# Two running sums of weights share tiles in another way, and the products that read them change places

## The chip, the cores and the metric

The kernel runs on one core of one Trainium2 chip. The metric is the device time of one execution in microseconds (us), the median of several. A core has TensorE (PE: matmuls into the accumulator banks of PSUM), VectorE (DVE), ScalarE (ACT), GpSimd (POOL) and SyncE (SP); the engines run their own queues in order and wait for each other by semaphores. DMA transfers are issued from an engine's queue, here SyncE's and GpSimd's.

## The reference

The reference is a decoder trunk of two layers on 512 tokens of width 1024, all in float32. Layer 0 mixes with differential and block-sparse attention, layer 1 with gated linear attention. Each layer ends with the part that the change touches, a feed-forward net of width 4096:

```python
def sqrelu_mlp(x, w1, w2):
    return jnp.square(jax.nn.relu(x @ w1)) @ w2

# in each layer
x = layer_norm(DEEPNORM_ALPHA * x + mix, ln_mix_g[l], ln_mix_b[l])
x = layer_norm(DEEPNORM_ALPHA * x + sqrelu_mlp(x, w1[l], w2[l]), ln_ffn_g[l], ln_ffn_b[l])
```

## The kernel before

**Split operands.** To keep float32 accuracy, each operand of a matmul is split into a high part (ScalarE, L117) and the rest (VectorE, L118). One product of two operands is then three matmuls: high by high, high by rest, rest by high. A weight tile is loaded whole into `raw` (four buffers, SyncE, L169), and its two parts go into buffers `w`: eight single ones, of which an entry of two takes two, and in the feed-forward stage one more double one. `entries` lists the splits in the order of use; `pump` starts the next one when a product has released its weights. `load_to` issues loads four ahead, as far as `raw` has a free buffer.

**The feed-forward net.** `ffn` works in four blocks of 1024 hidden columns. Blocks 0 to 2 multiply 2 x 2 matrices of sub-matrices with seven products in place of eight (Winograd's form), for the first matrix with `pair` (L872 to L918) on groups of columns, and for the second matrix with `second()` (L927 to L990). Block 3 has pairs too, and ends in plain products. Block 0 has one pair, blocks 1 to 3 have four each; a pair is 84 matmuls `pp` (L881). For a pair, `add_pair` forms sums of its two `raw` tiles on VectorE (L194, L187) and splits them; the results of a pair are added into `hb` in L815.

**Seven products.** In `second()` a product is 24 matmuls `pf` (L944): a left operand `ho` (a split of a quarter of `hb` or of a sum of such quarters: o11, o1, o12, o4, o2, o3, o22) by a right operand in two halves. The right operands are, with q00, q01, q10, q11 for the four quarters of the block of the second matrix: q00, q00+q01, q10, q11, q00+q01+q11, q01+q11 and the sum of all four. The results gather in bank pairs `A`, `B` and `C`: after a product, `into_x` (L403 or L405, VectorE) adds what the banks hold to x, and a later product adds on to the same banks. With `by_tokens` a product finishes the first 128 tokens before the second, and releases its two weight halves at its end; without it, it finishes and releases half by half. So a product on the banks of the one before it must wait for `into_x`.

**The sums.** The running sums of quarters are made by DMA, in tiles `ws` of 2 x 1024 columns (two of them, from the pool of eight large tiles that also holds `hb`). GpSimd issues a plain transfer (L225) and then transfers that add to what the tile holds (L230); `keep_in_program_order` keeps their order. `start_sums` runs at the start of a block and makes q00+q01 in the first tile and q01+q11 in the second. After a half of the first tile has been split, `summed` adds the next quarter to it: q11 behind the second product's split, q10 behind the fifth's. An add waits until what it adds to has landed, and until the split has read the tile.

**The order.** A planner at compile time orders each engine's instructions: of those that it believes to be ready it takes the one that stands first in the program, by durations of its own. That order is then fixed on each engine.

Of the kernel before, what the change touches and what calls it, by code (L numbers as in the profile page):

```python
# [16 lines left out]
ALU = mybir.AluOpType  # L17
AX = mybir.AxisListType

P = 128  # L20
# [27 lines left out]
def trunk(ctx, tc, a, out):  # L48
    nc = tc.nc
    V, A, G, PE = nc.vector, nc.scalar, nc.gpsimd, nc.tensor  # L50
# [9 lines left out]
    def bank(name="ps"):  # L60
        return psp.tile([P, 512], F32, tag="ps", name=name)
# [11 lines left out]
    def t8(name, shape=(P, NH, T), dt=F32):  # L73
        return pool["u"].tile(list(shape), dt, tag="u", name=name)

    def t4(name, shape=(P, 1024), dt=F32):
        return pool["h"].tile(list(shape), dt, tag="h", name=name)
# [38 lines left out]
    def split(h, l, src):  # L116
        A.activation(h, src, AF.Copy)  # L117
        V.tensor_tensor(l, src, h.bitcast(F32), op=ALU.subtract)  # L118
# [27 lines left out]
    def pump(n=1):  # L146
        while n and W["ready"] < len(entries) and room(entries[W["ready"]][1]):
            ready()
            n -= 1

    def nxt():
        if not ops:
            ready()
        c, h, l = ops.popleft()
        held.append(c)
        return c, h, l

    def release(c):
        held.remove(c)
        W[c[0]] -= c[1]  # L160
# [6 lines left out]
    def add_load(dst, src):  # L167

        loads.append(lambda: nc.sync.dma_start(dst(), src))  # L169
        return len(loads)  # L170

    def raw(key):
        def dst():
            got[key] = rp.tile([P, 1024], F32, tag="raw", name="raw")
            return got[key]
        return dst
# [36 lines left out]
    def quad(u, i, n, half):  # L213

        return wst[u + 4 * i + 2 * n + half]

    tsum = {}

    def start_sums(key):

        u = blocks[key]
        tsum[key] = [t8("ws", (P, 2, 1024)) for _ in range(2)]
        for t, i in zip(tsum[key], (0, 1)):
            for half in range(2):
                tc.keep_in_program_order(nc.gpsimd.dma_start(t[:, half], quad(u, 0, 1, half)))  # L225
            for half in range(2):
                add_quad(t[:, half], quad(u, i, i, half))

    def add_quad(t, src):
        tc.keep_in_program_order(nc.gpsimd.dma_start(t, src, accum_op=ALU.add))  # L230
# [3 lines left out]
    def add_block(u, key):  # L234

        blocks[key] = u

        def plain(i, n):
            r = []
            for half in range(2):  # L240
                k = add_load(raw((key, i, n, half)), quad(u, i, n, half))
                r.append((k, 2, lambda h, l, half=half: split(h, l, got.pop((key, i, n, half)))))
            return r

        def summed(m, then=None):
            def fn(half, h, l):
                t = tsum[key][m][:, half]
                split(h, l, t)
                if then:
                    add_quad(t, quad(u, *then, half))  # L250
            return [(len(loads), 2, lambda h, l, half=half: fn(half, h, l)) for half in range(2)]

        steps = (lambda: plain(0, 0), lambda: summed(0, (1, 1)), lambda: plain(1, 0), lambda: plain(1, 1),
                 lambda: summed(0, (1, 0)), lambda: summed(1), lambda: summed(0))
        return [e for st in steps for e in st()]

    def add_ffn(u, layer):
        for b in range(NB):
            add_units(u, PLAIN[b])
            first, second = [], []  # L260
            for j in range(PLAIN[b], FBLK, 2):
                first += add_pair(u + j)
            if b < NB - 1:
                second = add_block(u + FBLK, (layer, b))
            entries.extend(first + second)
            if b == NB - 1:
                add_units(u + FBLK, FBLK)
            u += 2 * FBLK
# [131 lines left out]
    def resid(t, h, ps, scale, acc=None, op=ALU.add):  # L400
        xs = x[:, t, h * 512:(h + 1) * 512]
        if scale is None and acc is None:
            V.tensor_tensor(xs, xs, ps, op=op)  # L403
        else:
            V.scalar_tensor_tensor(xs, xs, 1.0 if scale is None else scale, ps, op0=ALU.mult, op1=op,  # L405
                                   accum_out=None if acc is None else acc[t][:, h:h + 1])
# [192 lines left out]
    xs, ws, done = set(), [set(), set()], [set(), set()]  # L599
# [201 lines left out]
    steps = [diff_step(h, t) for h in range(NH) for t in range(NT)]  # L801
# [10 lines left out]
    def ffn(layer, last, nfirst, c0, t_last):  # L812
# [109 lines left out]
        def into_x(i, n, bs):  # L922
            for tt in range(2):
                resid(2 * i + tt, n, bs[tt], None if (i, n) in seen else ALPHA, op=ALU.subtract if n else ALU.add)
            seen.add((i, n))

        def second():  # L927


            c = {k: [bank("pf") for _ in range(2)] for k in "AC"}  # L930
            a11, a21, a12, a22 = H[0][:, 0], H[0][:, 1], H[1][:, 0], H[1][:, 1]

            def left(src, halves=False):
                h, l = (t4("ho", (P, 4, 256), F32R) for _ in range(2))
                for z in ((slice(0, 2), slice(2, 4)) if halves else (slice(0, 4),)):
                    split(h[:, z], l[:, z], src[:, z])
                return h, l

            def one(k, op, w, half, tt, first):
                r = [z.rearrange("p (j c) -> p j c", j=2) for z in w[1:]]  # L940
                for j in range(2):
                    l = [z[:, 2 * half + j, tt * P:(tt + 1) * P] for z in op]
                    for n, (x_, y_) in enumerate(((0, 0), (0, 1), (1, 0))):
                        PE.matmul(c[k][tt], l[x_], r[y_][:, j, :], start=first and half == j == n == 0,  # L944
                                  stop=half == j == 1 and n == 2, skip_group_check=True)

            def prod(k, op, first, by_tokens=False):
                if by_tokens:
                    w = [nxt() for _ in range(2)]
                    for tt in range(2):  # L950
                        for half in range(2):
                            one(k, op, w[half], half, tt, first)
                            if tt == 1:
                                release(w[half][0])
                                pump(2)
                    return
                for half in range(2):
                    w = nxt()
                    for tt in range(2):
                        one(k, op, w, half, tt, first)  # L960
                    release(w[0])
                    pump(2)

            o11 = left(a11, True)
            s = t4("s", (P, 4, 256))
            sub(s, a22, a21)
            o1 = left(s)
            prod("A", o11, True)
            into_x(0, 0, c["A"])
            o12 = left(a12)  # L970
            V.scalar_tensor_tensor(s, s, -1.0, a11, op0=ALU.mult, op1=ALU.subtract)
            V.scalar_tensor_tensor(a12, a12, -1.0, s, op0=ALU.mult, op1=ALU.subtract)
            prod("C", o1, True)
            into_x(1, 1, c["C"])
            o4 = left(a12)
            c["B"] = [bank("pf") for _ in range(2)]
            prod("B", o12, True)
            into_x(0, 0, c["B"])
            o2 = left(s)
            sub(a21, a11, a21)  # L980
            prod("C", o4, False)
            into_x(0, 1, c["C"])
            o3 = left(a21)
            prod("A", o2, False, True)
            into_x(0, 1, c["A"])
            o22 = left(a22)
            prod("A", o3, False, True)
            into_x(1, 1, c["A"])
            prod("A", o22, False, True)
            into_x(1, 0, c["A"])  # L990
# [7 lines left out]
        for b in range(NB):  # L998
# [3 lines left out]
            if not fin:  # L1002
                start_sums((layer, b))
            for n in range(0 if b else nfirst, PLAIN[b]):
                add_a(evac(n))
            if b == 0:
                ops_, third = right_operands()
# [5 lines left out]
            if not fin:  # L1013
                second()
                continue
# [398 lines left out]
```

## Time and profile before

| | us |
|---|---|
| median of 3 runs | 1190.36 (1188.38 to 1193.89) |
| profiled execution | 1192.47 |
| its span, first to last instruction | 1190.7 |

| engine | busy us | share |
|---|---|---|
| TensorE, matmuls | 1140.6 | 96% |
| TensorE, weight loads | 988.1 | 83% |
| VectorE | 867.8 | 73% |
| ScalarE | 622.8 | 52% |
| GpSimd | 112.2 | 9% |

The three runs and the profiled execution are of one program; the profiled execution's rows are used below. An engine's busy time is not enough to tell what sets the end: matmuls are pipelined, and a wait on an engine that has time left costs nothing. So the views that count are those of waits and the timelines of single stretches. Times in them are counted from the span's start. In layer 0, `second()` of blocks 0, 1 and 2 starts at 297, 385 and 470 us.

### The profile page before, as it was taken

How to read it: one execution, taken by the hardware profiler on the slowest of the kernel's cores; microseconds unless marked ns; L12 is line 12 of the kernel's file. 1: busy time of each engine (PE TensorE's matmuls, PEld its weight loads, DVE VectorE, ACT ScalarE, POOL GpSimd, SP SyncE). 2: the span in 40 equal slices, each digit the busy share in tenths (PEclk: the TensorE clock that was granted, in tenths of full speed). 3: DMA queues.
4: the chain of work that ended last, by engine and by line, in shares of the span. 5: the costliest groups of instructions: out<-in, count | busy, mean ns of one | idle time of the engine just before them, and what ended most of it. 6: DMA issues, size and time to landing. Idle time of an engine off the chain costs nothing.

```text
span 1190.7 us, 16757 instructions
## 1 busy us (share of the span) xinstructions
PE 1140.6 (96%) x6538; PEld 988.1 (83%) x6538; DVE 867.8 (73%) x1359; ACT 622.8 (52%) x1046; POOL 112.2 (9%) x136
## 2 busy tenths in 40 slices
PE   9999999999989999999999999999999899899997
PEld 6787776889779789799888888888987887887986
DVE  5677863578976986995657756486879679679846
ACT  6535466446646647566336433633564565564731
POOL 1132410010110010001010000000102002000000
PEclk9999999999999999999999999999999999899998
DMA  7512242073674675435232123401656566463331
GB/s 265 205 53 71 71 147 66 1 212 94 139 210 121 141 200 142 107 106 188 72 102 84 58 87 99 138 32 50 181 159 161 140 163 174 125 168 66 121 107 71
DMA packets 42735, 145.79 MB, mean 122 GB/s; under 512 B 5152, under 2 KB 6176, under 8 KB 42656
## 3 DMA queue, kind: packets, MB, share of 16 engines
q1 hardware_dynamic: 30640, 101.92, 26.3%
q0 software_dynamic: 12016, 42.80, 16.5%
q8 instruction: 51, 0.84, 0.3%
q14 instruction: 28, 0.23, 0.1%
HBM read 142.61 MB, written 2.10 MB: 122 GB/s over the span
## 4 chain that ended last, share of the span: by engine, by line
PE 79%; DVE 6%; ACT 6%; issue 4%; DMA 3%; POOL 1%; DVEq 0%; POOLq 0%; ACTq 0%
PE pp L881 20%; PE pf L944 15%; PE pf L280 4%; PE pf L279 4%; PE pf L281 4%; PE pb L279 4%; PE pb L280 4%; PE pb L281 3%; PE pa L279 3%; PE pa L281 3%; PE pa L280 3%; DMA raw<-in_wst 3%; ACT w L117 2%; DVE w L118 2%; PE pl L1212 1%
## 5 line engine op out<-in xcount | busy, mean ns | idle before, releaser
L118 DVE TENSOR_TENSOR w<-raw,w 128x1024 fp32r<-128x1024 f32 (+2 forms) x210 | 242.6, 1165 | 122.5 <-ACT w L117 99.4
L117 ACT ACTIVATE w<-raw 128x1024 fp32r<-128x1024 f32 (+2 forms) x210 | 205.7, 986 | 167.1 <-PE pf L944 26.9
L944 PE MATMUL pf<-w,ho 128*128 128x512 f32 x1008 | 234.9, 391 | 4.9 <-ACT ho L117 4.0
L944 PEld LDWEIGHTS pf<-w,ho 128*128 128x128 f32 x1008 | 187.4, 188 | 48.0 <-ACT ho L117 6.6
L881 PE MATMUL pp<-xTh,w 128*128 128x256 f32 x832 | 161.3, 286 | 9.3 <-ACT w L117 5.8
L881 PEld LDWEIGHTS pp<-xTh,w 128*128 128x128 f32 x832 | 135.6, 194 | 12.1 <-ACT w L117 7.5
L881 PE MATMUL pp<-T,w 128*128 128x256 f32 x936 | 127.1, 289 | 14.9 <-DVE hb L815 14.9
L881 PEld LDWEIGHTS pp<-T,w 128*128 128x128 f32 x936 | 119.2, 196 | 16.8 <-DVE hb L815 15.7
L881 PE MATMUL pp<-xTl,w 128*128 128x256 f32 x416 | 118.9, 286 | 0.0
L279 PE MATMUL pa<-xTh,w 128*128 128x512 f32 x264 | 106.0, 403 | 0.0
L281 PE MATMUL pa<-xTh,w 128*128 128x512 f32 x264 | 103.1, 391 | 0.0
L280 PE MATMUL pa<-xTl,w 128*128 128x512 f32 x264 | 103.0, 390 | 0.0
L881 PEld LDWEIGHTS pp<-xTl,w 128*128 128x128 f32 x416 | 81.0, 195 | 0.2
L230 POOL DMA_DIRECT2D ws<-in_wst x48 | 42.1, 877 | 400.5 <-DVE w L118 334.8
L279 PE MATMUL pb<-w,xTh 128*128 128x512 f32 x192 | 76.3, 401 | 1.0 <-ACT w L117 1.0
L280 PE MATMUL pb<-w,xTh 128*128 128x512 f32 x192 | 75.1, 391 | 0.4 <-DVE w L118 0.4
L281 PE MATMUL pb<-w,xTl 128*128 128x512 f32 x192 | 75.3, 392 | 0.0
L117 ACT ACTIVATE w<-ws 128x1024 fp32r<-128x1024 f32 x48 | 50.8, 1059 | 42.4 <-PE pf L944 41.6
L118 DVE TENSOR_TENSOR w<-ws,w 128x1024 fp32r<-128x1024 f32 x48 | 58.1, 1220 | 14.0 <-ACT w L117 9.2
L281 PEld LDWEIGHTS pa<-xTh,w 128*128 128x128 f32 x264 | 49.6, 188 | 10.6
L280 PEld LDWEIGHTS pa<-xTl,w 128*128 128x128 f32 x264 | 49.8, 188 | 9.2
L279 PEld LDWEIGHTS pa<-xTh,w 128*128 128x128 f32 x264 | 49.7, 189 | 9.1
(280 smaller groups left out, 2082.5 us busy)
## 6 DMA issues: line engine op xcount, KB each, us to landing
raw<-in_wst SPq DMA_DIRECT2D x178, 512.0 KB, 3.6
ws<-in_wst POOLq DMA_DIRECT2D x72, 512.0 KB, 6.0
xraw<-in_xT SPq DMA_DIRECT2D x8, 256.0 KB, 4.9
x<-in_x SPq DMA_DIRECT2D x4, 512.0 KB, 6.8
gb<-in_lng POOLq DMA_DIRECT2D x4, 512.0 KB, 5.6
gb<-in_lnb POOLq DMA_DIRECT2D x4, 512.0 KB, 6.5
out_x<-x SPq DMA_DIRECT2D x7, 256.0 KB, 2.0
tab<-in_rope SPq DMA_DIRECT2D x2, 512.0 KB, 5.2
```

Of the source, the lines that this page charges most:

```text
L117: A.activation(h, src, AF.Copy)
L118: V.tensor_tensor(l, src, h.bitcast(F32), op=ALU.subtract)
L230: tc.keep_in_program_order(nc.gpsimd.dma_start(t, src, accum_op=ALU.add))
L279: PE.matmul(o, l[0], r[0], start=first, stop=False)
L280: PE.matmul(o, l[0], r[1], start=False, stop=False)
L281: PE.matmul(o, l[1], r[0], start=False, stop=last)
L881: PE.matmul(o, w[x_], z[y_], start=first and k == n == 0, stop=k == 3 and n == 2, skip_group_check=True)
L944: PE.matmul(c[k][tt], l[x_], r[y_][:, j, :], start=first and half == j == n == 0, stop=half == j == 1 and n == 2, skip_group_check=True)
L1212: PE.matmul(pl[:, h * P:(h + 1) * P], z, z, start=True, stop=True)
```

## The change

`start_sums` makes q00+q01 in the first tile as before. The second tile is first a copy of the first by DMA, and then q11 is added to it: q00+q01+q11. Once the second product's operand has been split from the first tile, `third` writes q01 there anew and adds q11. After the second tile has been split, q10 is added to it, which makes the sum of all four. So the first tile is read for q00+q01 and q01+q11, the second for q00+q01+q11 and the sum of four.

The order of products changes to match: the product of o2 with q00+q01+q11 (banks `A`) comes fourth, no longer by tokens, and that of o4 with q11 (banks `C`) fifth. The other five keep their places. The negated sum in `a12` (L972) is formed after the second product's `into_x`, and o2 is split before o4.

```diff
     def start_sums(key):
 
         u = blocks[key]
-        tsum[key] = [t8("ws", (P, 2, 1024)) for _ in range(2)]
-        for t, i in zip(tsum[key], (0, 1)):
-            for half in range(2):
-                tc.keep_in_program_order(nc.gpsimd.dma_start(t[:, half], quad(u, 0, 1, half)))
-            for half in range(2):
-                add_quad(t[:, half], quad(u, i, i, half))
+        a1, a2 = tsum[key] = [t8("ws", (P, 2, 1024)) for _ in range(2)]
+        for half in range(2):
+            bring(a1[:, half], quad(u, 0, 1, half))
+        for half in range(2):
+            add_quad(a1[:, half], quad(u, 0, 0, half))
+        for half in range(2):
+            bring(a2[:, half], a1[:, half])
+        for half in range(2):
+            add_quad(a2[:, half], quad(u, 1, 1, half))
+
+    def bring(t, src):
+        tc.keep_in_program_order(nc.gpsimd.dma_start(t, src))
...
                 if then:
-                    add_quad(t, quad(u, *then, half))
+                    then(t, half)
...
-        steps = (lambda: plain(0, 0), lambda: summed(0, (1, 1)), lambda: plain(1, 0), lambda: plain(1, 1),
-                 lambda: summed(0, (1, 0)), lambda: summed(1), lambda: summed(0))
+        def third(t, half):
+            bring(t, quad(u, 0, 1, half))
+            add_quad(t, quad(u, 1, 1, half))
+
+        steps = (lambda: plain(0, 0), lambda: summed(0, third), lambda: plain(1, 0),
+                 lambda: summed(1, lambda t, half: add_quad(t, quad(u, 1, 0, half))),
+                 lambda: plain(1, 1), lambda: summed(0), lambda: summed(1))
...
             V.scalar_tensor_tensor(s, s, -1.0, a11, op0=ALU.mult, op1=ALU.subtract)
-            V.scalar_tensor_tensor(a12, a12, -1.0, s, op0=ALU.mult, op1=ALU.subtract)
             prod("C", o1, True)
             into_x(1, 1, c["C"])
-            o4 = left(a12)
+            V.scalar_tensor_tensor(a12, a12, -1.0, s, op0=ALU.mult, op1=ALU.subtract)
+            o2 = left(s)
             c["B"] = [bank("pf") for _ in range(2)]
             prod("B", o12, True)
             into_x(0, 0, c["B"])
-            o2 = left(s)
+            o4 = left(a12)
             sub(a21, a11, a21)
+            prod("A", o2, False)
+            into_x(0, 1, c["A"])
+            o3 = left(a21)
             prod("C", o4, False)
             into_x(0, 1, c["C"])
-            o3 = left(a21)
-            prod("A", o2, False, True)
-            into_x(0, 1, c["A"])
             o22 = left(a22)
             prod("A", o3, False, True)
             into_x(1, 1, c["A"])
```

## Rows read from the trace of the kernel before

**Rows 1.** The page's first part: busy us (share) x instructions.

```profile
PE 1140.6 (96%) x6538; PEld 988.1 (83%) x6538; DVE 867.8 (73%) x1359; ACT 622.8 (52%) x1046; POOL 112.2 (9%) x136
```

**Rows 2.** Waits of TensorE, whole span: us in total, times, longest.

```profile
PE pp L881 <- DVE hb L815: 14.9, 4, 4.3
PE pp L881 <- ACT w L117: 5.8, 4, 1.5
...
PE pp L881 <- DVE w L118: 3.5, 2, 1.7
```

**Rows 3.** Timeline of TensorE, 408 to 439: start, us, [idle before <-releaser].

```profile
408.68 5.60 PE L944 MATMUL pf<-w,ho 128*128 128x512 f32 x24
...
416.24 0.50 PE L881 MATMUL pp<-xTh,w 128*128 128x256 f32 x2 [1.73 <-DVE w L118]
...
417.06 11.07 PE L944 MATMUL pf<-w,ho 128*128 128x512 f32 x48
...
438.41 0.86 PE L881 MATMUL pp<-T,w 128*128 128x256 f32 x5 [2.62 <-DVE hb L815]
```

**Rows 4.** Timeline of VectorE, 400 to 439, same block.

```profile
401.75 1.21 DVE L118 TENSOR_TENSOR ho<-hb,ho 128x1024 fp32r<-128x1024 f32 x1
...
412.38 1.22 DVE L118 TENSOR_TENSOR ho<-hb,ho 128x1024 fp32r<-128x1024 f32 x1
...
416.10 1.28 DVE L403 TENSOR_TENSOR x<-x,pf 128x512 f32<-128x512 f32 x2
...
418.43 1.28 DVE L194 TENSOR_TENSOR s<-raw 128x512 f32<-128x512 f32 x2
...
434.60 0.69 DVE L194 TENSOR_TENSOR s<-raw 128x512 f32<-128x512 f32 x1 [3.17 <-DMA raw<-in_wst]
```

**Rows 5.** Single issues at 339.9, 388.0, 427.9, 428.5, 513.5: KB, us to landing.

```profile
raw<-in_wst SPq DMA_DIRECT2D x1, 512.0 KB, 7.8
...
raw<-in_wst SPq DMA_DIRECT2D x1, 512.0 KB, 4.7
...
raw<-in_wst SPq DMA_DIRECT2D x1, 512.0 KB, 6.7
...
raw<-in_wst SPq DMA_DIRECT2D x1, 512.0 KB, 9.9
...
raw<-in_wst SPq DMA_DIRECT2D x1, 512.0 KB, 3.5
```

**Rows 6.** Timeline of GpSimd, 380 to 442: its DMA issues.

```profile
385.75 0.87 POOL L230 DMA_DIRECT2D ws<-in_wst  x1 [2.14 <-DVE w L118]
...
404.40 0.87 POOL L230 DMA_DIRECT2D ws<-in_wst  x1 [2.60 <-DVE w L118]
413.90 1.09 POOL L225 DMA_DIRECT2D ws<-in_wst  x2 [8.63 <-DVE ho L118]
...
427.83 1.92 POOL L230 DMA_DIRECT2D ws<-in_wst  x2 [6.62 <-DMA ws<-in_wst]
```

**Rows 7.** Timeline of ScalarE, 407 to 414.

```profile
412.73 1.06 ACT L117 ACTIVATE w<-ws 128x1024 fp32r<-128x1024 f32 x1 [1.12 <-PE pf L944]
```

**Rows 8.** Issue to landing, L225 (24 plain transfers), then L230 (48 adds).

```profile
DMA to landing us min/median/max: 3.8/6.9/9.5
...
DMA to landing us min/median/max: 5.3/5.8/10.4
```

**Rows 9.** Timeline of TensorE, the start of `second()` in block 2.

```profile
470.43 2.91 PE L944 MATMUL pf<-w,ho 128*128 128x512 f32 x12
```

**Rows 10.** Windows: length, busy us of PE, PEld, DVE, ACT, POOL, PEclk, DMA share.

```profile
388.50:431.40 42.90, 40.45 (x193) 33.76 (x194) 42.12 (x49) 22.76 (x26) 7.48 (x10) 1.00 0.69 178
...
352.00:357.00 5.00, 4.99 (x30) 4.99 (x31) 3.20 (x5) 4.05 (x8) 0.00 (x0) 0.68 0.60 210
438.40:443.40 5.00, 4.99 (x41) 4.99 (x42) 3.60 (x6) 4.46 (x10) 0.00 (x0) 1.00 0.39 108
1022.10:1028.10 6.00, 5.97 (x29) 5.97 (x30) 3.45 (x6) 3.74 (x8) 0.00 (x0) 0.54 0.30 90
```

## The prediction, made blind

> **What bounds the kernel now.** The page's first part comes before anything else: TensorE is busy for 96% of the span, VectorE for 73% [rows 1]. A transfer, split or sum is worth something here only if it shortens TensorE's 50 us of idle time, so the next view is whom TensorE waited for [rows 2]. The feed-forward blocks hold 24 us of it: four waits for the adds to `hb` in L815 (14.9 us) and six for the first weight of a pair (5.8 + 3.5 us). No entry names a weight sum. That is the first thing to see: the tile `ws`, which the change rearranges, is not what TensorE waits for.
>
> The timelines place these waits. In `second()` of block 1, layer 0, the fifth product is the 24 matmuls from 408.68 to 414.28. Then a few matmuls of the next pair are slipped in, one of them waits 1.73 us for its weight, and the sixth product starts only at 417.06 [rows 3]. What slipped them in: the fifth product (bank `A`, o2) and the sixth (`A`, o3) add into the same banks, and between the two `into_x` must read them. VectorE reaches that L403 at 416.10, since a split of `ho` from 412.38 and weight splits stand ahead of it [rows 4]. There are six such gaps, 9.3 us, one for each block with a `second()` [rows 2].
>
> The other wait comes 8 us after the seventh product, which ends at 428 [rows 3]. VectorE stands at L194 for 3.17 us until a `raw` tile lands [rows 4]; the adds of L815 are behind it in VectorE's queue, and TensorE waits 2.62 us for those [rows 3]. That transfer (427.9) took 6.7 us, its like in block 0 (339.9) 7.8 us; at the start of block 3 (513.5), which makes no sums, one took 3.5 us [rows 5]. GpSimd's row shows what moved meanwhile: the last two adds of `start_sums`, from 427.83 [rows 6].
>
> **The change part by part.** *Sums.* Before, a block has 12 transfers of 512 KB: four plain and eight adds. After, 14: two plain ones of q01, two copies of `a1` into `a2`, two more of q01 in `third`, and still eight adds. On the readers' side this removes a tight step: the add issued at 404.40 behind the fifth product's split lands within 5.8 us (median), at 410.2, and its reader, the split at 412.73, waited for TensorE and not for it [rows 6 to 8]. There were 2.5 us to spare, so relaxing this gains 0. The new distances are longer: `a2` is split for the fourth product and again for the seventh, three products of 5.6 us later; `a1` for the second and the sixth, 22 us apart, in which a plain transfer (3.8 to 9.5 us) and an add (5.3 to 10.4) fit even at their worst [rows 8]. In `third` the second half's transfer stands on GpSimd's queue behind the first half's add, about 4 us; only sums wait there.
>
> *The copy in start_sums.* It waits for `a1`'s add, and `a2`'s add waits for it; on GpSimd's queue only the second copy and the adds stand behind. The trace has no copy from one on-chip tile to another. By the nearest rows it takes 3.8 us (a plain transfer alone) to 9.5 (one in a crowd) [rows 8]; I take 4.5, near the first, since one other transfer at most is ahead of it. The chain is then 4.5 + 6 + 4.5 + 6 = 21 us from its first issue. Before, the last adds are issued 14 us after it, 413.90 to 427.83 [rows 6], and need 6 to 10 more [rows 8]: it ends about when it did. The first reader of `a2` comes after the four pairs, 428 to 470 [rows 3, 9]; they hide the chain with 20 us to spare, and all four links at their upper ends (9.5 + 10.4, twice: 40 us) would just be covered. Without the pairs all 21 us would be paid. Exposed is only what these transfers do to the `raw` loads.
>
> *The order of products.* o2 moves to fourth, o4 to fifth. `into_x` can now read `A` during a whole product `C`, 5.6 us, and the sixth product can follow the fifth at once, provided that o3 is split: it was at 413.6, and the fifth product ended at 414.28 [rows 3, 4]. The fourth product needs o2 where it needed o4; o4's split ended at 402.96, just ahead of the fourth product's start at 403.1 (408.68 less 5.6) [rows 3, 4]. o2 comes from `s`, one operation earlier than `a12`, so it is no later: 0. L972 behind an `into_x` delays o4, which has a product more: 0. The fourth and fifth products now both release their weights by halves; one slot comes free 1.4 us earlier, a help inside the next term.
>
> *Term 1, the six gaps.* If they go entirely, TensorE saves 9.3 us, and in the four blocks with an L815 wait the slipped-in matmuls, about 1 us each, fill time in which TensorE waited anyway: upper end 13. But VectorE is busy for 42.12 of the 42.90 us from 388.50 to 431.40 [rows 10]. In the old order it can be 0.78 us earlier and no more, and a TensorE that comes early waits for L815 instead: lower end 6 x 0.78 = 4.7. The order need not stay: before some L403s VectorE does sums of a later pair (L194 at 418.43) [rows 4] that can wait. I take 7, midway between 4.7 and 9.3.
>
> *Term 2, the L815 waits.* They end with the landing of a `raw` tile. At its issue, two adds and another `raw` were under way; after the change, the tail of the second copy, an add or two and the same `raw`. Bounds: it lands as without sums, 3.5 us (all 14.9 us go), or as the worst `raw` of the stretch (428.5), 9.9 us, 3.2 more at each of four places (+13) [rows 5]. Nothing in the count of transfers favours either strongly; I take 0.5 us each, 2 us. The Trainium skill has a rule that speaks against even this: in "DMA: Bandwidth & Descriptors", section "Queues, rings and completion order", each DMA engine goes round the queues that have work, packet by packet, so how many transfers wait in one queue would not matter to the other; by that rule this term is 0 and the sum 2 us poorer. The trace agrees only in part: beside a single add (385.75) a `raw` (388.0) took 4.7 us, beside two 6.7 [rows 5, 6].
>
> *Term 3, the clock.* After the long waits the granted clock lay between its two levels of 2.4 and 1.2 GHz: 0.68 over 5 us and 0.54 over 6, which is 1.6 and 2.8 us lost; after the 2.62 us wait it stayed at 1.00 [rows 10]. The fourth place counts as the first: 6.0 us in all. Waits somewhat shorter give back a part: I take 0.5 us (bounds: 6 gained, 2 lost).
>
> Sum: -7 - 2 - 0.5 = -9.5 us. The profiled execution took 1192.47 us, 1190.7 of them span; after it would be 1183.0. The median of the three runs lies 2.1 us below that execution, so I predict 1181.
>
> **The rivals.**
> *VectorE is the bound (A).* The gaps go and the time returns as longer waits for L815; 0.78 us a block is left, 1185 to 1188, say 1187. For it: the busy time in [rows 10]. Against it: part of the work in the way can come later.
> *Every wait goes (B).* `raw` lands in 3.5 us, VectorE keeps up, the clock stays: 9.3 + 14.9 + 6 = 30 us, 1160. Against it: `a2`'s adds are still issued about when the `raw` is.
> *Slower (C).* The copy reads and writes the same memory that `raw` is written to, and the serial chain shifts its transfers onto that one load. If it lands in over 9 us instead of 6.7 to 7.8, the four waits grow by 3.2 each: +13, +2 of clock, less term 1's 7: +8, 1198. For it: a `raw` issued 0.6 us later already took 9.9 [rows 5]. Below 8 us it costs nothing that counts.
> *It does nothing (D).* The sums were not late, and the compile-time planner keeps matmuls of a pair, with a weight that is late, ahead of the sixth product: 1190, give or take 3.
>
> **How the numbers follow.** Forecast 0.42, A 0.25, B 0.10, C 0.10, D 0.13. A change under 0.5% (6 us) can't be told from none in this kernel. Faster: nearly all of the forecast, B and a little of A, 0.53. Slower: C and a sliver of D, 0.11. The rest, 0.36, is no difference. The range leaves out B and C: from 1168 (term 1 at 13, terms 2 and 3 at 9 together) to 1193 (D's upper end).
>
> **What would show it.** After the change the six waits of `pp` for a weight are gone and the sixth product follows the fifth without a gap; waits for L815 remain at the same four places with 2 to 4 us; the copies land in 4 to 6 us; no split waits for `ws`. If the gaps are gone and L815's waits have grown by as much, A holds; if that `raw` lands in over 9 us, C. I am wrong from the start if matmuls of a pair still stand between the fifth and the sixth product, or if a fourth product waits for `ho`.

## The result, and the profile after

| us | before | after |
|---|---|---|
| median | 1191.57 (4 runs, 1188.38 to 1193.89) | 1176.72 (4 runs, 1175.88 to 1177.74) |
| profiled execution | 1192.47 | 1176.95 |
| its span | 1190.7 | 1175.2 |

The ratio of the medians is 0.9878, 95% interval 0.9851 to 0.9904: 14.9 us or 1.2% faster, 4.3 us below the predicted 1181. The lines of the kernel after stand 11 lower: L815 is L826, L881 is L892, L944 is L955; plain transfers and copies of `ws` are L233, adds L236.

A stretch is named here by the block whose `second()` opens it; the pairs behind that `second()` belong to the next block. The page's first part answers to [rows 1], the waits of TensorE in the feed-forward stage (us in total, times, longest) to [rows 2].

```profile
PE 1140.5 (97%) x6538; PEld 988.6 (84%) x6538; DVE 867.2 (74%) x1359; ACT 622.5 (53%) x1046; POOL 119.5 (10%) x148
```

```profile
PE pp L892 <- DVE hb L826: 8.8, 4, 3.6
PE pf L955 <- ACT ho L117: 4.0, 6, 0.8
PE ds L1269 <- DVE S L1271: 0.7, 1, 0.7
```

TensorE, VectorE and ScalarE are busy for as long as before, GpSimd 7.3 us longer; what went is idle time. The two entries of `pp` for a weight are gone (5.8 + 3.5 us), and the waits for the adds to `hb` fell from 14.9 to 8.8 us. The timeline of TensorE in block 1's stretch, layer 0 (start, us, [idle before <-releaser]) answers to [rows 3]:

```profile
388.69 29.32 PE L955 MATMUL pf<-w,ho 128*128 128x512 f32 x128
...
418.32 5.63 PE L955 MATMUL pf<-w,ho 128*128 128x512 f32 x24
...
424.74 3.04 PE L892 MATMUL pp<-T,w 128*128 128x256 f32 x24
...
443.04 1.70 PE L892 MATMUL pp<-T,w 128*128 128x256 f32 x12 [0.83 <-DVE hb L826]
```

Before, a few `pp` and a wait of 1.73 us stood between the fifth product and the sixth. Now the 128 matmuls from 388.69 (16 of the first product's stand ahead of them) run through to the end of the sixth, with no `pp` among them; the row of 418.32 is the seventh. What is left of the wait for `hb` comes at 443, 19 us after the seventh product and one pair later than before. VectorE shows why (answers to [rows 4]):

```profile
431.45 0.75 DVE L826 TENSOR_TENSOR hb<-p,pp 128x256 f32<-128x256 f32 x2
...
432.48 0.69 DVE L194 TENSOR_TENSOR s<-raw 128x512 f32<-128x512 f32 x1
...
438.09 0.69 DVE L194 TENSOR_TENSOR s<-raw 128x512 f32<-128x512 f32 x1 [1.52 <-DMA raw<-in_wst]
...
442.24 0.75 DVE L826 TENSOR_TENSOR hb<-p,pp 128x256 f32<-128x256 f32 x2
```

Before, the L194 that waited for a late `raw` was the third pair's, and the first pair's adds to `hb` stood behind it. After, those adds (431.45) stand ahead of the third pair's L194 (432.48), which finds its tile there. The L194 that waits, 1.52 us, is now the fourth pair's, and the second pair's adds (442.24) stand behind it.

**The account.** One window, called the stage below, runs from the first `second()` in layer 0 to the plain products of block 3 in layer 1: 297.43 to 1138.60 before, 300.03 to 1123.07 after. Columns as in [rows 10], with the kernel before first:

```profile
297.43:1138.60 841.17, 810.48 (x4822) 716.98 (x4821) 637.33 (x921) 447.34 (x704) 61.43 (x92) 0.99 0.46 127
```

```profile
300.03:1123.07 823.04, 808.00 (x4822) 715.91 (x4821) 636.75 (x921) 447.11 (x704) 69.02 (x104) 0.99 0.49 138
```

The stage got 18.1 us shorter. TensorE's idle time in it (length less busy) fell from 30.69 to 15.04, by 15.65: the gaps' 9.3, the `hb` waits' 6.1, and 0.2. Its busy time fell by 2.5, with the same 4822 matmuls. The missing 2.6 us between 18.1 and the span's 15.5 lie ahead of the stage, which began at 300.03 and not at 297.43, though the engines run the same instructions in the same order up to 231 us. The granted clock differs (after):

```profile
100.00:140.00 40.00, 37.18 (x182) 29.96 (x181) 30.51 (x57) 20.30 (x45) 14.59 (x8) 0.96 0.22 65
...
180.00:231.00 51.00, 48.68 (x267) 38.47 (x266) 21.20 (x54) 29.90 (x76) 0.00 (x0) 0.97 0.13 39
```

Before:

```profile
100.00:140.00 40.00, 37.26 (x191) 30.19 (x190) 30.45 (x57) 20.31 (x45) 14.58 (x8) 1.00 0.19 63
180.00:228.60 48.60, 46.73 (x265) 37.30 (x266) 19.75 (x52) 28.52 (x73) 0.00 (x0) 1.00 0.11 33
```

In the other profiles the stage began between 297.2 and 300.3 us, with the old sums as with the new, so this is a difference of executions. Profiles are therefore compared below by their waits and by the time from the stage's start to the end of the span: 893.3 us before, 875.1 after.

### The profile page after: what moved, and what is told of

It is laid out like the page before. It is cut to its first block, busy times and chain, and to the rows that moved or that the text cites. A ratio compares the mean times of both kernels' runs of the same rounds, so it can differ in the third digit from the quotient of the medians.

```text
span 1175.2 us, 16786 instructions
## 1 busy us (share of the span) xinstructions
PE 1140.5 (97%) x6538; PEld 988.6 (84%) x6538; DVE 867.2 (74%) x1359; ACT 622.5 (53%) x1046; POOL 119.5 (10%) x148
## 4 chain that ended last, share of the span: by engine, by line
PE 80%; DVE 6%; ACT 5%; issue 4%; DMA 3%; POOL 1%; DVEq 0%; ACTq 0%; POOLq 0%
PE pf L955 18%; PE pp L892 18%; PE pf L291 4%; PE pf L290 4%; PE pf L292 4%; PE pb L290 4%; PE pb L291 4%; PE pb L292 4%; PE pa L290 3%; DMA raw<-in_wst 3%; PE pa L291 3%; PE pa L292 3%; DVE w L118 2%; ACT w L117 2%; PE pl L1223 1%
## 5 line engine op out<-in xcount | busy, mean ns | idle before, releaser
L955 PE MATMUL pf<-w,ho 128*128 128x512 f32 x1008 | 234.6, 391 | 4.9 <-ACT ho L117 4.0
L955 PEld LDWEIGHTS pf<-w,ho 128*128 128x128 f32 x1008 | 187.4, 188 | 48.1 <-ACT ho L117 6.6
L892 PE MATMUL pp<-xTh,w 128*128 128x256 f32 x832 | 159.8, 285 | 0.0
L892 PEld LDWEIGHTS pp<-xTh,w 128*128 128x128 f32 x832 | 134.7, 194 | 0.5
L892 PE MATMUL pp<-T,w 128*128 128x256 f32 x936 | 126.3, 289 | 8.8 <-DVE hb L826 8.8
L892 PEld LDWEIGHTS pp<-T,w 128*128 128x128 f32 x936 | 118.7, 195 | 11.1 <-DVE hb L826 9.6
L892 PE MATMUL pp<-xTl,w 128*128 128x256 f32 x416 | 118.4, 285 | 0.0
L892 PEld LDWEIGHTS pp<-xTl,w 128*128 128x128 f32 x416 | 80.6, 194 | 0.5
L118 DVE TENSOR_TENSOR w<-ws,w 128x1024 fp32r<-128x1024 f32 x48 | 58.1, 1221 | 13.6 <-ACT w L117 8.8
L292 PEld LDWEIGHTS pa<-xTh,w 128*128 128x128 f32 x264 | 50.0, 189 | 10.8
L233 POOL DMA_DIRECT2D ws<-in_wst x24 | 15.1, 632 | 429.3 <-DVE w L118 192.5
L117 ACT ACTIVATE w<-s 128x512 fp32r<-128x512 f32 x52 | 32.6, 628 | 48.8 <-DVE s L194 27.9
```

The source lines that it names most:

```text
L233: tc.keep_in_program_order(nc.gpsimd.dma_start(t, src))
L292: PE.matmul(o, l[1], r[0], start=False, stop=last)
L892: PE.matmul(o, w[x_], z[y_], start=first and k == n == 0, stop=k == 3 and n == 2, skip_group_check=True)
```

## Experiments

What is apart: (a) does the new order of products carry the gain, or do the new sums; (b) why did the `hb` waits shrink; (c) what sets the rest of them; (d) is VectorE the next bound. Each run was timed beside the kernel before on the same chip. The waits, and the time from the stage's start to the end, are those of one profiled execution.

| | sums | order of products | median us | ratio to before, 95% | waits for `hb`, us | stage's start to end, us |
|---|---|---|---|---|---|---|
| before | old | old | 1191.4 to 1192.3 | 1 | 14.9 | 893.3 |
| e2 | new | old | 1183.83 | 0.9942 [0.992, 0.9964] | 7.5 | 881.0 |
| e1, e1_again | old | new | 1170.61, 1172.11 | 0.9816 [0.9791, 0.984], 0.9834 [0.9811, 0.9856] | 6.3, 6.2 | 870.4, 870.5 |
| after, after_again | new | new | 1176.72, 1175.99 | 0.9878 [0.9851, 0.9904], 0.9871 [0.9847, 0.9895] | 8.8, 8.4 | 875.1, 871.8 |
| e3 | new | new, fourth by tokens | 1174.93 | 0.9864 [0.9829, 0.9899] | 11.8 | 880.9 |
| e4 | new, adds and copies of the start left out | new | 1164.21 | 0.9773 [0.9747, 0.9798] | none | 862.4 |
| e5 | new, second tile held back | new | 1162.25 | 0.9752 [0.9728, 0.9776] | none | 861.7 |
| e6 | old, second tile held back | new | 1162.27 | 0.9755 [0.9733, 0.9777] | none | 861.8 |
| e7 | old, second tile held back | old | 1175.89 | 0.9863 [0.9831, 0.9895] | 1.9 | 876.6 |
| e8 | old | old, no `into_x` ahead of the sixth | 1173.37 | 0.9842 [0.9806, 0.9878] | 4.0, and 4.0 for `u` | 871.5 |

Edits are given against the kernel after, unless said.

**e1_order_only, and e1_again: the order alone.**

```diff
-        a1, a2 = tsum[key] = [t8("ws", (P, 2, 1024)) for _ in range(2)]
...
+        for t, i in zip(tsum[key], (0, 1)):
...
-        steps = (lambda: plain(0, 0), lambda: summed(0, third), lambda: plain(1, 0),
-                 lambda: summed(1, lambda t, half: add_quad(t, quad(u, 1, 0, half))),
-                 lambda: plain(1, 1), lambda: summed(0), lambda: summed(1))
+        steps = (lambda: plain(0, 0), lambda: summed(0, lambda t, half: add_quad(t, quad(u, 1, 1, half))),
+                 lambda: plain(1, 0), lambda: summed(0, lambda t, half: add_quad(t, quad(u, 1, 0, half))),
+                 lambda: plain(1, 1), lambda: summed(1), lambda: summed(0))
```

> The new order of products with the old sums (second tile made from two plain loads, first tile read for three products). Order theory: the six gaps between the fifth and the sixth product vanish, and TensorE, coming earlier, also shifts VectorE's planned order, so L815's waits are 7 to 11 us as in the changed kernel (8.8): 1176 to 1180 us. Sums theory (the shorter waits for L815 come from the lighter start of the sums): the gaps vanish but L815's waits stay near 14.9 us: 1181 to 1184 us.

> The changed kernel as it is, beside the next three on the same chip: 1175 to 1179 us, with 7 to 11 us of waits for L815's adds.

> The new order with the old sums once more, on the same chip as the changed kernel. If the new sums cost time under the new order (copy and serial chain keep the adds moving while later raw loads are due): 4 to 8 us less than the changed kernel, 1168 to 1173 us. If the 6 us between the two in earlier runs came from the chip: within 2 us of the changed kernel.

Measured: 1170.61, below both expected ranges, and on another chip 1172.11 beside 1175.99 for the kernel after, 3.9 us less where 4 to 8 were expected. Of nine times of e1, eight (1166.7 to 1172.21) lie below all ten of the kernel after (1173.31 to 1181.6); the ninth is 1175.54. So the order alone brings 20 us, and with the new sums beside it the time is 4 to 6 us longer. Not all of this is shown to be the sums' price. From the stage's start on, the profiled executions differ by 4.7 us in the first pair and by 1.3 in the second (two executions of the kernel after differ by 3.3 themselves); the rest lies ahead of the stage, where the granted clock of the two stretches shown above was 0.96 and 0.97 in both executions of the kernel after and 1.00 in both of e1. In the stage it is the waits for `hb` that differ (e1_again first, then after_again):

```profile
PE pp L885 <- DVE hb L819: 6.2, 4, 2.8
```

```profile
PE pp L892 <- DVE hb L826: 8.4, 4, 3.0
```

Apart from block 0's own pair in each layer, TensorE, VectorE and ScalarE run the same order of instructions in both kernels, so here it is the transfers' times that differ. The reason offered is the serial chain in `start_sums`. In block 0's stretch, layer 0, GpSimd issues its last adds at 339.61 and 342.02 in e1_again, and at 343.19 and 346.02 in after_again, where each waits for its copy (GpSimd's timelines, same order):

```profile
339.61 0.89 POOL L233 DMA_DIRECT2D ws<-in_wst  x1 [6.49 <-DMA ws<-in_wst]
342.02 0.88 POOL L233 DMA_DIRECT2D ws<-in_wst  x1 [1.53 <-DMA ws<-in_wst]
```

```profile
343.19 0.90 POOL L236 DMA_DIRECT2D ws<-in_wst  x1 [2.19 <-DMA ws<-ws]
346.02 0.90 POOL L236 DMA_DIRECT2D ws<-in_wst  x1 [1.93 <-DMA ws<-ws]
```

Under the new order the load that VectorE waits for is the fourth pair's, here issued at 345.25 in e1_again and 347.50 in after_again, 47.8 us from the stage's start in both. By the same count the adds come 1.3 and 1.8 us later in after_again (the stage itself began 2.25 us later), and the load takes 7.4 us and not 6.3. The four such loads took 7.4, 6.5, 8.6 and 8.6 us in after_again and 6.3, 8.5, 6.9 and 7.1 in e1_again: three are slower with the new sums, one is faster, so the chain is not shown to be the reason in every place.

**e2_sums_only: the sums alone.**

```diff
         steps = (lambda: plain(0, 0), lambda: summed(0, third), lambda: plain(1, 0),
+                 lambda: plain(1, 1),
                  lambda: summed(1, lambda t, half: add_quad(t, quad(u, 1, 0, half))),
-                 lambda: plain(1, 1), lambda: summed(0), lambda: summed(1))
+                 lambda: summed(0), lambda: summed(1))
...
-            prod("A", o2, False)
-            into_x(0, 1, c["A"])
-            o3 = left(a21)
             prod("C", o4, False)
             into_x(0, 1, c["C"])
+            o3 = left(a21)
+            prod("A", o2, False, True)
+            into_x(0, 1, c["A"])
```

> The new sums (copy by DMA, two tiles shared in the new way) with the old order of products. Order theory: the gaps stay at 9.3 us and L815's waits near 14.9 us, so it takes as long as the kernel before: 1189 to 1194 us. Sums theory: the gaps stay, L815's waits fall by about 6 us: 1184 to 1187 us. A copy that hurts would show as over 1195 us.

Measured: 1183.83 over 12 runs, 7.6 us faster than before and at the edge of what the sums theory expected. The gaps stay, the waits for `hb` halve:

```profile
PE pp L892 <- DVE hb L826: 7.5, 6, 1.9
PE pp L892 <- ACT w L117: 5.8, 4, 1.5
...
PE pp L892 <- DVE w L118: 3.5, 2, 1.7
```

Its single `raw` loads issued at 338.0, 342.0 and 427.0 (KB, us to landing):

```profile
raw<-in_wst SPq DMA_DIRECT2D x1, 512.0 KB, 4.3
...
raw<-in_wst SPq DMA_DIRECT2D x1, 512.0 KB, 4.7
...
raw<-in_wst SPq DMA_DIRECT2D x1, 512.0 KB, 5.1
```

The first two are the third pair's in block 0's stretch, the last is that pair's second load in block 1's; before, they took 6.3, 7.8 and 6.7 us [rows 5 for the last two]. Here too, apart from block 0's own pair, the three engines' order is that of the kernel before, so it is the transfers' times that make the difference. In block 0's stretch the chain fits as the reason: its last adds are issued at 343.69 and 344.94, when those loads have been issued or have landed, and the fourth pair's take 6.2 and 6.8. In block 1's an add (426.82) does move beside the load. That the same delay is a gain under the old order, where the third pair's load is the tight one, and a loss under the new, where it is the fourth's, is the reading that fits; it was not tested by itself. The two parts of the change don't add up: 7.6 and 20 alone, 15 together.

**e3_fourth_by_tokens: the release of weights by halves.**

```diff
-            prod("A", o2, False)
+            prod("A", o2, False, True)
```

> The changed kernel with its fourth product (o2) by tokens again, so that its two weight halves are released only at its end. If the order alone does it: within 2 us of the changed kernel, 1175 to 1179 us. If the earlier release by halves carries a part: the splits of the sixth and seventh product's weights come 1.4 us later and 1 to 1.5 us a block return, 1182 to 1186 us.

Measured: 1174.93 (1170.68 to 1181.45), within 2 us of the kernel after. The way in which the fourth product gives its weights back carries nothing that these runs can tell. (The profiled execution is the slowest of the four, 1181.45, with 11.8 us of waits, though TensorE, VectorE and ScalarE run exactly the order of the kernel after.)

**e4_light_start: `start_sums` with its plain transfers only.**

```diff
         for half in range(2):
             bring(a1[:, half], quad(u, 0, 1, half))
         for half in range(2):
-            add_quad(a1[:, half], quad(u, 0, 0, half))
-        for half in range(2):
-            bring(a2[:, half], a1[:, half])
-        for half in range(2):
-            add_quad(a2[:, half], quad(u, 1, 1, half))
+            bring(a2[:, half], quad(u, 1, 1, half))
```

> The changed kernel whose start_sums makes only four plain transfers: the two adds to the first tile, the two copies and the two adds to the second are left out, so both tiles lack terms. If L815's remaining waits (8.8 us) come from raw loads that share the DMA engines with the sums: raw loads land in 3.4 to 4.5 us throughout, these waits fall under 1 us, the clock keeps 1.00 and it takes 1162 to 1167 us. If VectorE itself is the bound there: the waits stay at 6 to 9 us, 1173 to 1177 us.

Measured: 1164.21, 12.5 us below the kernel after, and no wait for `hb` at all. The four loads of the third and fourth pair in block 0's stretch, layer 0, land in:

```profile
DMA to landing us min/median/max: 3.3/3.5/4.7
```

So the adds and copies of `start_sums`, moving while the pairs' loads do, are the cause of all that was left of these waits. The planner also put a few operations of VectorE elsewhere here (TensorE's order is unchanged), but the order of the kernel after would not have waited either: its four loads took 7.6, 6.5, 9.3 and 8.0 us, VectorE waited 2.49, 1.52, 4.22 and 3.18 us for them, so a load of 4.8 to 5.1 us would have been early enough, and here the four take 4.2 to 4.7. VectorE did not become the bound.

**e5_copy_later: the same transfers, later.** Copy and second adds are held back in blocks 1 and 2 until the second pair is done, by a one-column copy on GpSimd that reads `hb`; nothing is left out.

```diff
+    def rest_of_sums(key, after=None):
+        u = blocks[key]
+        a1, a2 = tsum[key]
+        if after is not None:
+            tc.keep_in_program_order(G.tensor_copy(gate_, after))
...
                 pair(n // 2, ops_)
+                if b and not fin and n == PLAIN[b] + 2:
+                    rest_of_sums((layer, b), H[0][:, 0, n // 2, 0:1])
```

> The changed kernel, but in blocks 1 and 2 the copy into the second tile and the adds to it are held back until the second pair is done, by a one-column copy on GpSimd that reads that pair's result. If the sums' transfers beside the raw loads of the third and fourth pair make the remaining waits for L815: those fall under 2 us in total, 1162 to 1168 us, as with the transfers left out. If the held-back copy comes too late for the fourth product: splits wait for ws, and it takes 1172 us or more.

Measured: 1162.25, 13.7 us below the kernel after and 1.2% better; the fastest of all, level with e6. GpSimd's timeline in block 0's stretch, layer 0, whose pairs are block 1's (the gate is L234):

```profile
358.43 0.58 POOL L234 COPY gate<-hb 128x1 f32<-128x1 f32 x1 [26.63 <-DVE w L118]
358.99 1.11 POOL L241 DMA_DIRECT2D ws<-ws  x2
362.17 0.90 POOL L244 DMA_DIRECT2D ws<-in_wst  x1 [2.08 <-DMA ws<-ws]
```

The loads issued from 335 to 352 and from 415 to 440:

```profile
DMA to landing us min/median/max: 3.4/3.6/4.1
...
DMA to landing us min/median/max: 3.5/3.8/4.5
```

TensorE's waits in the stage:

```profile
PE pf L963 <- ACT ho L117: 4.0, 6, 0.8
PE ds L1281 <- DVE S L1283: 0.6, 1, 0.6
```

Between the profiled executions of after_again and e5, 12.6 us apart in span, all is accounted for: 8.4 of waits, 1.7 of clock in the stage (0.72 over the 6 us from 1015 in after_again), and 2.5 ahead of the stage (299.70 against 297.23), where the edit changes nothing. In the stage it is 10.1 us. Two windows of block 1's stretch, `second()` and the pairs behind it (columns as in [rows 10]), speak to VectorE as a bound:

```profile
377.50:417.60 40.10, 39.20 (x175) 31.87 (x174) 38.30 (x45) 23.13 (x27) 6.90 (x9) 1.00 0.70 175
417.60:457.70 40.10, 40.10 (x333) 39.95 (x332) 30.54 (x45) 25.98 (x48) 3.62 (x6) 1.00 0.61 186
```

VectorE is as full in `second()` as in the kernel after (38.30 of 40.11 us from 383.69), and TensorE is idle for 0.9 us all the same. In the pairs VectorE has 9.6 us left and TensorE no idle time at all.

**e6_order_later and e7_before_later: held back under either order, with the old sums.** e6 is e1, e7 the kernel before, each with this edit:

```diff
+    def one_sum(key, i, after=None):
+        u, t = blocks[key], tsum[key][i]
+        if after is not None:
+            tc.keep_in_program_order(G.tensor_copy(gate_, after))
...
                 pair(n // 2, ops_)
+                if b and not fin and n == PLAIN[b] + 2:
+                    one_sum((layer, b), 1, H[0][:, 0, n // 2, 0:1])
```

> The new order with the old sums, the second tile's four transfers held back in the same way until the second pair is done. By the same reasoning 1162 to 1168 us, equal to the run with the held-back copy within 2 us: then the way in which the tiles are shared has no price of its own once the transfers are out of the way. If the sharing itself matters, the two differ by 4 us or more.

> The kernel before (old order, old sums), with the second tile's four transfers held back in blocks 1 and 2 until the second pair is done. If the raw loads that share the DMA engines with the sums make L815's waits here too: those (14.9 us) and the clock's loss after them (6 us) go, the six gaps between the fifth and sixth product (9.3 us) stay: 1169 to 1174 us. If VectorE is the bound there, as the rival in the prediction has it: L815's waits stay over 8 us, 1183 to 1192 us.

Measured: e6 1162.27, the same as e5; once the second tile is out of the way of the loads, it makes no difference which sums share one. e7 1175.89, just above the 1169 to 1174 that was expected, and 16 us faster than before with the old order and old sums. Its waits show what the old order leaves:

```profile
PE pp L888 <- ACT w L117: 5.8, 4, 1.5
...
PE pp L888 <- DVE w L118: 3.5, 2, 1.7
PE pp L888 <- DVE hb L822: 1.9, 2, 1.7
```

The gaps' 9.3 us stay, the waits for `hb` are down to 1.9. From e7 to e6 the new order gives 13.6 us, of which the gaps and these waits are 11.2.

**e8_no_read: the gap without the order.** The kernel before, without the `into_x` between the fifth and the sixth product.

```diff
             prod("A", o2, False, True)
-            into_x(0, 1, c["A"])
```

> The kernel before without the reading of bank A between the fifth and the sixth product (the additions into x after o2's product are left out, so those results count wrongly). If that reading makes the six gaps: the sixth product follows the fifth at once, pp's waits for a weight (9.3 us) vanish, 1178 to 1184 us. If the late weight of the pair makes them, not the bank: the pair's matmuls stay between and the gaps with them, 1188 to 1193 us.

Measured: 1173.37, below the 1178 to 1184 that was expected. TensorE in block 1's stretch, layer 0, and its waits:

```profile
387.26 34.75 PE L944 MATMUL pf<-w,ho 128*128 128x512 f32 x152 [0.15 <-DVE ho L118]
```

```profile
PE pp L881 <- DVE hb L815: 4.0, 5, 1.2
...
PE pp L881 <- ACT u L900: 4.0, 2, 2.2
```

The fifth and sixth product run through, the waits for a weight are gone, and the waits for `hb` fall to 4.0 us (with 4.0 for `u`, which was no entry before), although neither the sums nor the order of the products changed. So the read of `A` between the two products makes the gap: without it there is none. And closing the gap by itself changes the rest of the engines' order enough to shrink the waits for `hb`. VectorE has 12 L403s of 0.68 us less here, 8 us, so how much of the 19 us is due to the gap alone is not told by this run.

## Why the prediction was right, and where it was not

**What bounds the kernel: right.** Idle time of TensorE in two kinds of places went, the engines' work did not. No split waits for `ws` in the profiles before and after. (In after_again one on ScalarE does, 1.32 us at 896.91; TensorE does not wait for it.)

**Term 1, the gaps: -7 taken, -9.3 measured.** Mechanism and places were right, the size too cautious. The bound of 0.78 us a block came from VectorE's busy share within one block [rows 10], taken as if its order stayed. It did not: the third pair's L194 now stands behind the first pair's adds.

**Term 2, the waits for `hb`: -2 taken, -6.1 measured; the step that failed.** The sign was right, the size and the mechanism were not. I asked only how much faster the same `raw` lands beside other transfers. It does land sooner, in layer 0 in 6.5 and 6.2 us (issued at 341.0 and 423.8) against 7.8 and 6.7 [rows 5]. But that is not what the waits shrank by: with the old sums and the new order they shrink further, to 6.3 and 6.2 us (e1). Under the new order the first pair's adds stand ahead of the third pair's L194, so another load, the fourth pair's, became the one that VectorE waits for, and it has more time: VectorE comes to it some 5 us after its issue, where it came to the third pair's 3.3 to 3.5 us after (in [rows 4, 5]: at 431.43, issued at 427.9). Some 1.6 us at each of four places is about the 6.1. Those loads, issued at 347.8, 431.6, 920.9 and 1007.5 after, took:

```profile
raw<-in_wst SPq DMA_DIRECT2D x1, 512.0 KB, 7.6
...
raw<-in_wst SPq DMA_DIRECT2D x1, 512.0 KB, 6.5
...
raw<-in_wst SPq DMA_DIRECT2D x1, 512.0 KB, 9.3
...
raw<-in_wst SPq DMA_DIRECT2D x1, 512.0 KB, 8.0
```

They were no faster than 6.7 and 7.8 us, and the waits shrank all the same. "The same four places" was wrong by one pair, and "2 to 4 us" each became 0.83 to 3.58. The shift comes with the closed gap (in e8, too, VectorE waits for a fourth pair's load, 3.88 us until 437.77), and I had priced the two terms apart. The rule of the Trainium skill that the prediction weighed, "DMA: Bandwidth & Descriptors", section "Queues, rings and completion order", is neither borne out nor refuted: no two of these loads differ only in how many transfers wait in the other queue.

**The sums: 0 on the readers' side held; their price lies with the `raw` loads.** I had the chain end about when it did before; it ends later (last add of block 0's stretch issued at 347.97 against 342.14, which is 47.9 and 44.7 us from the stage's start). `second()` reads the tile much later, so that is covered. What the sums do to the `raw` loads I had priced within term 2 as a gain of 2 us. By themselves they bring -7.6 us under the old order (e2), and under the new one they go with waits that are 2.2 and 2.5 us longer (after against e1).

**The copy: 4.5 taken, 4 to 6 expected.** The 12 copies took 2.8 to 7.3 us, 5.8 in the median; with those of blocks 1 and 2 held back (e5), 4.0:

```profile
ws<-ws POOLq DMA_DIRECT2D x12, 512.0 KB, 5.8
```

```profile
ws<-ws POOLq DMA_DIRECT2D x12, 512.0 KB, 4.0
```

**Term 3, the clock: -0.5 taken, about -1.4 measured**, in four stretches behind the waits of 1.87, 0.83, 3.58 and 2.48 us (after, answers to [rows 10]):

```profile
360.00:365.00 5.00, 4.62 (x26) 4.62 (x27) 2.59 (x5) 3.70 (x7) 0.00 (x0) 0.66 0.59 210
442.00:447.00 5.00, 4.17 (x35) 3.96 (x35) 3.58 (x7) 3.95 (x8) 0.00 (x0) 1.00 0.59 210
935.00:941.00 6.00, 5.80 (x27) 5.80 (x28) 3.42 (x6) 4.62 (x9) 0.00 (x0) 0.51 0.43 167
1020.00:1026.00 6.00, 5.51 (x46) 5.51 (x47) 4.54 (x8) 5.50 (x11) 0.00 (x0) 1.00 0.53 175
```

Lost: 0.34 x 5 + 0.49 x 6 = 4.6 us, against 6.0 before. This size is partly that of one execution: after_again lost only 1.7 in the stage. TensorE's busy time in the stage fell by 2.5; the other 1.1 are not placed.

**Rivals.** *VectorE is the bound (A)* fell: the waits shrank with the gaps, and in e4 to e6 they are gone with VectorE as busy as ever. *Every wait goes (B)* named a mechanism that exists, 1162 in e5 and e6 against 1160 forecast for it; the change doesn't bring it, because its adds stay beside the loads, as the prediction's point against B had it. *Slower (C)*: a `raw` did take 9.3 us in one place, and under the new order the time is longer with the new sums, but only by part of the gain; the price falls on the next pair's load, not on the one that the rival named. *It does nothing (D)* fell with the first timeline.

That the total came out within 4.3 us of the forecast is partly luck. Terms 1 to 3 gave 16.8 us, and the stage got 18.1 shorter, where 9.5 was forecast. Two things hid half of that error. The profiled execution lost 2.6 us ahead of the stage; it took 1176.95, 6.0 below the 1183.0 that the terms gave. And the 2.1 us by which the median lay below the profiled execution before, subtracted in the forecast, were only 0.2 after.

## What to carry to other kernels

A bank that must be read between two products that both add to it made a gap of 1.5 to 1.7 us each time here; put a product on other banks between them, and then look through the compile-time order again, because closing a gap moves which operation is stuck behind which on another engine. Transfers that nobody needs soon are not free if they share time with loads that are needed at once: hold them back with a small operation that depends on the work that should be done first (here 13.7 us between medians, 10.1 of them in the stage, for one column of a copy). Two parts of one change that meet at the same loads are measured apart and together; their gains need not add up.

## What the runs showed that was not expected

The length of a wait does not decide by itself what becomes of TensorE's clock: in the kernel after, it was granted 0.66 over 5 us behind a wait of 1.87 us, and 1.00 behind one of 2.48 us, as behind the 2.62 us before [rows 3, 10]. Why was not tested.

A 512 KB load that takes 3.3 to 4.7 us when the running sums keep away took 6.5 to 9.3 beside them in the four places where VectorE waited for one: here the neighbours, not the size, set when it landed.

The granted clock ahead of the stage was 0.96 and 0.97 in one execution and 1.00 in another, over unchanged instructions. That is worth some 2.6 us, so the spans of single profiles of this kernel cannot carry differences below about 3 us; the time from the stage's start on is free of this part, but still differed by 3.3 us between two executions of the kernel after.
